# Three row tiles of p @ W_ple_proj computed before v, another order of the products of W_o, and W_up opened by token halves in six chunks

## The chip, the cores and the metric

The kernel runs on one core of a Trainium2 chip. Its engines are TensorE (PE, matmuls; its loads of the stationary operand are shown as PEld), VectorE (DVE), ScalarE (ACT), GpSimd (POOL) and SyncE (SP, which here only issues DMAs). Each engine works through its own instructions in a fixed order and waits for others by semaphores. The metric is the device time of one execution in microseconds (us).

## What is computed

One layer of a decoder: 512 tokens of width 1024, all in float32.

```python
h = rms_norm(x, g_pre_mix)
q, k, v, cb, cc, cu, ga, gc = split(h @ w_in)
y_attn = stick_breaking_attention(q, k, v) @ w_attn_out
y_conv = (cb * causal_depthwise_conv(cc * cu, w_conv)) @ w_conv_out
mixed = (sigmoid(ga + b) * y_attn + sigmoid(gc + b) * y_conv) @ w_o
x = x + rms_norm(mixed, g_post_mix)
f = square(relu(rms_norm(x, g_pre_mlp) @ w_up)) @ w_down      # 1024 -> 4096 -> 1024
x = x + rms_norm(f, g_post_mlp)
x = x + sigmoid(rms_norm(x, g_ple) @ w_ple_gate) * (p @ w_ple_proj)   # p: 512 x 256
```

## The kernel before

**Products.** Each float32 product is made of three matmuls (`mm3`, lines 93 to 95 before, 97 to 99 after): both operands are split into a high part of type fp32r and the rest (`split`: a cast on ACT, line 64 before and 68 after, then a subtraction on DVE, line 65 before and 69 after), and high x high, high x low and low x high are added up in a PSUM bank. A weight chunk therefore needs a DMA into one of four raw buffers (pool `raws`), a cast on ACT and a subtraction on DVE before PE can use it, and the raw buffer is free after the subtraction. PSUM has eight banks, each of 128 x 512.

**Order.** PE and SP run in the order of the source. On ACT, DVE and POOL a scheduler that estimates times sets a fixed order when the program is built; `tc.high_priority(n)` shifts an instruction in its list and `tc.issue_after(i)` keeps one behind another. Each DMA takes one of eight completion semaphores in turn (both SP's and ACT's DMAs), and its issue waits until the DMA that had the same one has landed.

**The head.** SP loads x in four row tiles of 128 tokens (`xin`) and the v columns of w_in in four pieces (`vr`). PE passes the time with transposes of the identity (`warmup`, line 187 before, 208 after), spreads g_pre_mix over the partitions with eight small matmuls (line 228 before, 278 after), transposes the scaled x (`head_turn`, line 206 before, 227 after), and multiplies it with v's columns (`v_mm`). ACT squares x (line 125 before, 129 after), POOL takes the inverse root, DVE scales (`head_scale`, line 196 before).

**W_o.** `mixed @ w_o` is done in 2 x 2 blocks with seven products P1 to P7 in place of eight (a Strassen scheme), each of 24 matmuls of 512 columns in two halves, P6 added onto the bank of P1, P5 onto that of P6, P3 onto that of P5, P4 onto that of P7. Before a product goes onto a bank, ACT copies out what the bank holds (`wo_done`). P3 completes token tiles 0 and 1, P4 completes tiles 2 and 3. After that each tile goes through a chain (`chain_in`, `chain_add`, `chain_out`: square on ACT, inverse root on POOL, multiply and add on DVE, twice), ends in `hn1`, and is transposed on PE by `turn2` (line 570 before) into h2, the input of W_up.

**p @ w_ple_proj.** It does not depend on the rest until the last step. In the kernel before it stands between P4 and W_up: 48 matmuls of 512 columns (`pt`, `wpb`), with `turn2(0)` and `turn2(1)` among them; eight transposes of p stand after the first half of P7. The result goes to DRAM (`pps`) and is read back at the end.

**W_up.** W_up has 32 chunks of 128 columns; chunk c and c + 16 go together. Chunks 0, 16, 1, 17 are done for tokens 0 to 255 first, then for 256 to 511, so that PE can start before tiles 2 and 3 are through their chain (`turn2(2)`, `turn2(3)` stand in the first half). Then chunks 2 and 18 follow with all 512 tokens, and the other 26 chunks in a Strassen scheme of seven products of 12 matmuls with 256 columns for each pair (`up_steps`, `up_mm`), whose weights pass through sums on DVE (lines 781 to 786).

Of the kernel before, what the change touches and what calls it, by code (L numbers as in the profile page):

```python
# [8 lines left out]
F32 = mybir.dt.float32  # L9
# [16 lines left out]
LATE = 150  # L26
EPS = 1e-6
# [6 lines left out]
def hybrid_block(ctx, tc, x, p, g_pre_mix, w_in, b_gate, w_conv, w_attn_out, w_conv_out, w_o,  # L34
# [135 lines left out]

    load_x(0)
# [75 lines left out]
    split_v(1)  # L247
# [317 lines left out]
    def turn2(t):  # L565
        tok = slice(t * P, (t + 1) * P)
        for g in range(2):
            ps = bank()
            for i in range(4):
                nc.tensor.transpose(ps[:, i * P:(i + 1) * P], hn1[t][g][:, i * P:(i + 1) * P], ident)  # L570
            p3 = ps.rearrange("p (a b) -> p a b", b=P)
            hold[:] = split(h2[0][g][:, :, tok], h2[1][g][:, :, tok], p3)
            nc.scalar.copy(hf[t // 2][:, g, :, (t % 2) * P:(t % 2 + 1) * P], p3)
# [5 lines left out]
    ORDER = (1, 2, 6, 7, 5, 3, 4)  # L579
# [29 lines left out]
    pf = {}  # L609

    def load_pp():
        pf[0] = raws.tile([P, NT, 256], F32, tag="raw", name="raw")
        nc.sync.dma_start(pf[0], p[0].rearrange("(t p) d -> p t d", p=P))
        for kk in range(2):
            raw = raws.tile([P, D], F32, tag="raw", name="raw")
            nc.sync.dma_start(raw, w_pp[kk * P:(kk + 1) * P, :])
            split(wpb[kk][:, 0], wpb[kk][:, 1], raw)

    def turn_p():
        for kk in range(2):  # L620
            ps = bank()
            for t in range(NT):
                nc.tensor.transpose(ps[:, t * P:(t + 1) * P], pf[0][:, t, kk * P:(kk + 1) * P], ident)
            split(pt[:, kk], pt[:, 2 + kk], ps)
# [20 lines left out]
    def wo_done(n, t):  # L645
# [8 lines left out]
        elif n == 6:  # L654
            nc.scalar.copy(oc[t + 2][:, 0], ps)
        elif n == 5:
            nc.scalar.copy(oc[t + 2][:, 1], ps)
            nc.vector.tensor_tensor(oc[t + 2][:, 1], oacc[7, t], oc[t + 2][:, 1], op=ALU.add)
        elif n == 3:
            chain_in(t)  # L660
            if t == 1:
                chain_add(0)
                chain_add(1)
                with tc.issue_after(norm[1][1].ins):
                    chain_out(0)
# [24 lines left out]

    pp = [bigt([P, 2, D], F32, "pp") for _ in range(2)]
    for t in range(NT):
        tok = slice(t * P, (t + 1) * P)
        for h_ in range(2):
            cs = slice(h_ * 512, (h_ + 1) * 512)
            ps = bank()
            for kk in range(2):
                mm3(ps, pt[:, kk, tok], pt[:, 2 + kk, tok], wpb[kk][:, 0, cs], wpb[kk][:, 1, cs], kk == 0, kk == 1)
            nc.scalar.copy(pp[t // 2][:, t % 2, cs], ps)
            if (t, h_) in ((0, 1), (1, 0)):  # L700
                turn2(t)
                with tc.issue_after(hold[0].ins), tc.issue_after(hold[1].ins):
                    chain_in(2 + t)
                    chain_add(2 + t)
                    if t == 1:
                        chain_out(2)
                        chain_out(3)
        if t % 2 == 1:
            nc.scalar.dma_start(pps[t // 2], pp[t // 2])
# [116 lines left out]
    for c in (2, 2 + NJ):  # L826
        relu2(c, proj(wcols(w_up, c * P), hm))
# [28 lines left out]
    NI = NJ // 2  # L856
    LEFT = {1: (0, 0), 2: (0, 1), 6: (0, 0), 7: (0, 0), 5: (1, 0), 3: (0, 1), 4: (1, 1)}
# [180 lines left out]
```

## Time and profile before

| what | value |
|---|---|
| median of three runs | 733.33 us (733.2 to 734.62) |
| the profiled execution, its own time | 733.09 us |
| span of that execution, first to last instruction | 731.2 us |
| PE busy | 722.3 us, 99% of the span |
| DVE, ACT, POOL busy | 541.5, 390.4, 110.7 us |
| DMA | 134.38 MB, mean 184 GB/s |

The span leaves out 1.9 us that lie around the instructions. PE's busy time counts from the start of a matmul to its modelled end; since matmuls overlap, 99% says that PE is seldom without an instruction, not that it is at its peak.

### The profile page before, as it was taken

To read this page: it belongs to the slowest core of one execution; us is meant where nothing else is said; L and a number is where in the kernel's file an instruction comes from. 1 tells how busy PE (TensorE), PEld (TensorE's weight loads), DVE (VectorE), ACT (ScalarE), POOL (GpSimd) and SP (SyncE) were. 2 spreads that over 40 slices of the span, in tenths; PEclk is the share of its full clock that TensorE was granted. 3 is DMA by queue.
4 is the path that set the end of the run, shared out by engine and by line. 5 is a ranking of instruction groups with operands and counts; after the bars stand their busy time and mean duration, and the time that the engine had idled before them with its cause. 6 is when DMAs were issued, how large, how long until landed. Compare 5 with 4: busy or idle time off the path is not lost.

```text
span 731.2 us, 10295 instructions
## 1 busy us (share of the span) xinstructions
PE 722.3 (99%) x3964; PEld 626.7 (86%) x3964; DVE 541.5 (74%) x642; ACT 390.4 (53%) x604; POOL 110.7 (15%) x128
## 2 busy tenths in 40 slices
PE   8999999999999999999999999999999999999997
PEld 7888888888888888888999999999988888888886
DVE  5768877879593744978789878876799878369762
ACT  6255455452422222675767667756867476356431
POOL 1106060524353352001100000000000000002100
PEclk9999999999999999999999999999999999999999
DMA  8495717166979989725533344423455766577211
GB/s 317 158 325 151 232 57 228 33 230 200 283 249 293 298 251 336 268 78 176 202 103 108 97 125 121 128 73 103 149 169 188 232 234 221 183 239 283 118 57 58
DMA packets 114233, 134.38 MB, mean 184 GB/s; under 512 B 4196, under 2 KB 82824, under 8 KB 113160
## 3 DMA queue, kind: packets, MB, share of 16 engines
q1 hardware_dynamic: 113592, 129.53, 55.4%
q10 hardware_dynamic: 592, 4.20, 1.4%
q8 instruction: 31, 0.51, 0.3%
q14 instruction: 18, 0.15, 0.1%
HBM read 110.64 MB, written 23.07 MB: 183 GB/s over the span
## 4 chain that ended last, share of the span: by engine, by line
PE 93%; DVE 3%; DMA 2%; ACT 1%; issue 1%; DVEq 0%
PE ps L93 29%; PE ps L95 29%; PE ps L94 29%; DMA raw<-in_w_up_dram 2%; PE ps L391 1%; PE ps L377 1%; PE ps L343 1%; DVE us L65 1%; PE ps L206 0%; PE ps L146 0%; PE ps L187 0%; PE ps L570 0%; ACT us L64 0%; DMA grow<-in_g_pre_mix_dram 0%; DVE s L781 0%
## 5 line engine op out<-in xcount | busy, mean ns | idle before, releaser
L93 PE MATMUL ps<-h1h,whi 128*128 128x512 f32 x288 | 113.3, 393 | 0.0
L95 PE MATMUL ps<-h1h,wlo 128*128 128x512 f32 x288 | 112.2, 390 | 0.0
L94 PE MATMUL ps<-h1l,whi 128*128 128x512 f32 x288 | 112.2, 389 | 0.0
L64 ACT CAST whi<-raw 128x1024 fp32r<-128x1024 f32 (+1 forms) x72 | 58.7, 845 | 68.9 <-DMA raw<-in_w_in_dram 52.0
L65 DVE TENSOR_TENSOR w<-raw,w 128x1024 fp32r<-128x1024 f32 x62 | 75.0, 1221 | 25.0 <-ACT w L64 16.7
L65 DVE TENSOR_TENSOR wlo<-raw,whi 128x1024 fp32r<-128x1024 f32 (+1 forms) x72 | 73.2, 1049 | 22.0 <-ACT whi L64 19.7
L64 ACT CAST w<-raw 128x1024 fp32r<-128x1024 f32 x62 | 64.8, 1052 | 41.6 <-DMA raw<-wsum 17.2
L93 PE MATMUL ps<-w,sb 128*128 128x512 f32 x216 | 84.1, 389 | 0.0
L95 PE MATMUL ps<-w,sb 128*128 128x512 f32 x216 | 84.0, 389 | 0.0
L94 PE MATMUL ps<-w,sb 128*128 128x512 f32 x216 | 84.0, 389 | 0.0
L138 POOL TENSOR_TENSOR rs<-ms,mhalf 128x1 f32<-128x1 f32 x20 | 16.7, 838 | 419.1 <-DVE ms L134 361.2
L93 PEld LDWEIGHTS ps<-h1h,whi 128*128 128x128 f32 x288 | 54.1, 188 | 11.4
L95 PEld LDWEIGHTS ps<-h1h,wlo 128*128 128x128 f32 x288 | 54.1, 188 | 11.3
L94 PEld LDWEIGHTS ps<-h1l,whi 128*128 128x128 f32 x288 | 54.1, 188 | 10.9
L93 PE MATMUL ps<-h2h,us 128*128 128x256 f32 x208 | 59.1, 284 | 0.4 <-DVE tmp L814 0.4
L94 PE MATMUL ps<-h2l,us 128*128 128x256 f32 x208 | 58.8, 283 | 0.0
L95 PE MATMUL ps<-h2h,us 128*128 128x256 f32 x208 | 58.8, 283 | 0.0
L65 DVE TENSOR_TENSOR us<-raw,us 128x1024 fp32r<-128x1024 f32 x39 | 47.4, 1220 | 11.0 <-ACT us L64 11.0
L64 ACT CAST us<-raw 128x1024 fp32r<-128x1024 f32 x39 | 40.2, 1049 | 17.3 <-DVE raw L786 10.2
L94 PEld LDWEIGHTS ps<-w,sb 128*128 128x128 f32 x216 | 40.5, 188 | 8.5
L95 PEld LDWEIGHTS ps<-w,sb 128*128 128x128 f32 x216 | 40.5, 188 | 8.4
L93 PEld LDWEIGHTS ps<-w,sb 128*128 128x128 f32 x216 | 40.5, 188 | 8.3
(221 smaller groups left out, 1718.8 us busy)
## 6 DMA issues: line engine op xcount, KB each, us to landing
raw<-in_w_in_dram SPq DMA_DIRECT2D x36, 512.0 KB, 7.3
w<-in_w_down_dram SPq DMA_DIRECT2D x32, 512.0 KB, 4.5
wsum<-w SPq DMA_DIRECT2D x32, 512.0 KB, 3.4
raw<-in_w_up_dram SPq DMA_DIRECT2D x32, 512.0 KB, 4.3
raw<-wsum SPq DMA_DIRECT2D x32, 512.0 KB, 5.4
raw<-in_w_down_dram SPq DMA_DIRECT2D x24, 512.0 KB, 4.3
raw<-in_w_ple_gate_dram SPq DMA_DIRECT2D x8, 512.0 KB, 6.1
w<-in_w_o_dram SPq DMA_DIRECT2D x6, 512.0 KB, 6.7
```

The source lines that it names most:

```text
L64: a = nc.scalar.copy(hi, src)
L65: b = nc.vector.tensor_tensor(lo, src, hi.bitcast(F32), op=ALU.subtract)
L93: nc.tensor.matmul(ps, lh, rh, start=start, stop=False, skip_group_check=onto)
L94: nc.tensor.matmul(ps, lh, rl, start=False, stop=False, skip_group_check=onto)
L95: nc.tensor.matmul(ps, ll, rh, start=False, stop=stop, skip_group_check=onto)
L138: nc.gpsimd.tensor_tensor(r, m, mhalf, op=ALU.pow)
L343: nc.tensor.matmul(ps[h][:, c0:c0 + n], st[r, a, qb * P:(qb + 1) * P], st[r, b, 0:n], start=i == 0, stop=i == 2)
L377: nc.tensor.transpose(ps[:, c0 + (qb - kb) * P:c0 + (qb - kb + 1) * P], w[:, o:o + P], ident)
L391: nc.tensor.matmul(ps[:, kb * P:S], lhs, wt[i][:, c0:c0 + n], start=(kb == 0 and i == 0), stop=(kb == NT - 1 and i == 1))
```

## The change

- **Head.** p's first three row tiles and all of w_ple_proj are loaded first, ahead of x and v. PE transposes p's tiles (line 246) and multiplies tiles 0, 1 and 2 (`pp_head`, 36 matmuls of 512 columns) before `head_turn(0)`. ACT copies the six banks out and issues three stores to DRAM (line 264). The identity transposes fall from 8 + 12 + 3 to 8 + 4.
- **W_o.** The order becomes P1 P2 P6 P5 P3 P7 P4; weights are prepared three half products ahead, not four. P7 is copied to `tmp` and added from there.
- **Late tile.** Tile 3 of p and w_ple_proj are loaded again during W_o; two transposes after P5 and 12 matmuls after P4 (`pp_late`). `turn2(0)` stands in the middle of P4, `turn2(1)` right after it.
- **W_up.** Chunks 2 and 18 join the four that open by token halves. `turn2(2)` stands after the fourth chunk, `turn2(3)` after the fifth. The copies to `hf` get a lower priority.

```diff
@@ head @@
+AHEAD = 3
+URG = 300
+PUT = 40
+WARM = 4
...
+    load_p(0)
+    for kk in range(2):
+        nc.sync.dma_start(ppr[kk], w_pp[kk * P:(kk + 1) * P, :])
     load_x(0)
+    load_v(0)
+    load_p(1)
     nc.scalar.dma_start(grow[0:NK, 0:P], g_pre_mix.rearrange("o (a b) -> (o a) b", b=P))
     load_x(1)
-    for i in range(4):
+    for i in range(1, 4):
         load_v(i)
...
+    def turn_p(hi, lo, src, n):
+        ps = bank()
+        for kk in range(2):
+            for t in range(n):
+                nc.tensor.transpose(ps[:, (n * kk + t) * P:(n * kk + t + 1) * P], src(t)[:, kk * P:(kk + 1) * P], ident)
+        return split(hi, lo, ps[:, 0:2 * n * P].rearrange("p (a b) -> p a b", a=2))
...
+    def pp_mm(ts, stat, w, to):
+        ps = {(t, h_): bank() for t in ts for h_ in range(2)}
+        for kk in range(2):
+            if kk == 1 and ts[0] == 0:
+                turn_pair(1)
+            for t, h_ in ps:
+                cs = slice(h_ * 512, (h_ + 1) * 512)
+                mm3(ps[t, h_], *(s[:, kk] for s in stat(t)), w[kk][0][:, cs], w[kk][1][:, cs], kk == 0, kk == 1)
+        for t, h_ in ps:
+            nc.scalar.copy(to(t)[:, h_ * 512:(h_ + 1) * 512], ps[t, h_])
+        for t in ts:
+            nc.scalar.dma_start(pps[t // 2][:, t % 2, :], to(t))
...
     warmup(8)
+    turn_pair(0)
...
-    warmup(12)
+    warmup(WARM)
     xs = [xin[t // 2][:, t % 2, :] for t in range(NT)]
-    with tc.issue_after(gdone.ins):
+    for kk in range(2):
+        for h_ in range(2):
+            cs = slice(h_ * 512, (h_ + 1) * 512)
+            ready = split(wpb[kk][0][:, cs], wpb[kk][1][:, cs], ppr[kk][:, cs])
+    pp_head(0, 1)
+    with tc.issue_after(gdone.ins), tc.issue_after(ready[0].ins), tc.issue_after(ready[1].ins):
         rs = {0: rstd_of([xs[0]])}
     scaled = head_scale(0, rs[0])
+    with tc.issue_after(ready[0].ins), tc.issue_after(scaled.ins):
+        split_v(0)
+        last = split_v(1)
     with tc.issue_after(scaled.ins):
         rs[1] = rstd_of([xs[1]])
+    pp_head(2)
     ps0 = head_turn(0)
...
-    warmup(3)
+    vps = [bank(), bank()]
+    v_mm(0, vps[0], 0)
@@ W_o @@
-    ORDER = (1, 2, 6, 7, 5, 3, 4)
+    ORDER = (1, 2, 6, 5, 3, 7, 4)
...
         elif n == 6:
-            nc.scalar.copy(oc[t + 2][:, 0], ps)
+            with tc.high_priority(URG):
+                nc.scalar.copy(oc[t + 2][:, 0], ps)
         elif n == 5:
             nc.scalar.copy(oc[t + 2][:, 1], ps)
-            nc.vector.tensor_tensor(oc[t + 2][:, 1], oacc[7, t], oc[t + 2][:, 1], op=ALU.add)
+        elif n == 7:
+            c = tm()
+            nc.scalar.copy(c, ps)
+            nc.vector.tensor_tensor(oc[t + 2][:, 1], c, oc[t + 2][:, 1], op=ALU.add)
...
-    THEN = {(1, 0): save_sums, (2, 0): load_xr, (2, 1): load_pp, (7, 0): turn_p}
+    THEN = {(1, 0): save_sums, (2, 0): load_xr, (6, 0): load_pp, (5, 1): turn_late,
+            (3, 1): lambda: h2_tiles(), (7, 0): lambda: load_wu(0), (7, 1): lambda: load_wu(NJ),
+            (4, 0): lambda: turn2(0), (4, 1): lambda: (turn2(1), pp_late(), load_wu(1), load_wu(1 + NJ))}
@@ W_up @@
     for half in range(2):
         ns = slice(half * 256, (half + 1) * 256)
-        for c in (0, NJ, 1, 1 + NJ):
+        for c in (0, NJ, 1, 1 + NJ, 2, 2 + NJ):
...
-            if half == 0 and c in (NJ, 1):
-                turn2(3 - c // NJ)
-                if c == NJ:
+            if half == 0 and c in (1 + NJ, 2):
+                turn2(2 if c == 1 + NJ else 3)
+                if c == 1 + NJ:
                     held = list(hold)
...
-    for c in (2, 2 + NJ):
-        relu2(c, proj(wcols(w_up, c * P), hm))
```

**Where it moves instructions.** PE at the start of the program, before: identity, gain, identity, then x's first tile and v (`vh`, `vl` are the split columns of v, `h1h`, `h1l` the split x).

```order
L187 MATMUL ps<-ident 128x128 x8
L228 MATMUL ps<-gsp 128x128 x8
L187 MATMUL ps<-ident 128x128 x12
L206 MATMUL ps<-ident,xin 128x128 x8
L93 MATMUL ps<-vh,h1h 128x512
L94 MATMUL ps<-vl,h1h 128x512
L95 MATMUL ps<-vh,h1l 128x512
L187 MATMUL ps<-ident 128x128 x3
L206 MATMUL ps<-ident,xin 128x128 x8
```

PE at the same place, of the change, up to the first product of p (`wpb` is the split w_ple_proj, `w_108` and `w_109` the split transposed p).

```order
L208 MATMUL ps<-ident 128x128 x8
L246 MATMUL ps<-ident,raw 128x128 x4
L278 MATMUL ps<-gsp 128x128 x8
L208 MATMUL ps<-ident 128x128 x4
L97 MATMUL ps<-wpb,w_108 128x512
L98 MATMUL ps<-wpb,w_108 128x512
L99 MATMUL ps<-wpb,w_109 128x512
```

Such threes stand there twelve times, with two transposes of p's third tile after the fourth; only then x's first tile follows. ACT in the head, of the change, from the first v cast (`vh`) on:

```order
L68 CAST vh<-vr 128x512
L262 COPY pp<-ps 128x512 x2
L264 DMA pps_116<-pp 128x1024
L262 COPY pp<-ps 128x512
L68 CAST vh<-vr 128x512
L264 DMA pps_116<-pp 128x1024
L262 COPY pp<-ps 128x512 x2
L68 CAST h1h<-ps 128x4x128
L264 DMA pps_117<-pp 128x1024
L68 CAST vh<-vr 128x512
L68 CAST h1h<-ps 128x4x128
```

Before, the cast of x's first tile (`h1h`) followed the two squares of x on ACT directly; now six copies and two stores stand between them, and a third store stands right behind it. ACT between P5 and the end of P7, of the change (L733 copies P5's two banks, L129 squares P3's banks and the rows of x, L736 copies P7's banks, `w_3087` and `w_3113` are P4's weights, `whi` W_up's):

```order
L733 COPY w_2861<-ps 128x512
L733 COPY w_2871<-ps 128x512
L68 CAST pt<-ps 128x256
L68 CAST w_3018<-ot 128x1024
L68 CAST w_3034<-ot 128x1024
L68 CAST w_3087<-ot 128x1024
L129 ACTIVATE junk,ss<-ps 128x512
L68 CAST whi<-raw 128x512
L129 ACTIVATE junk,ss<-ps 128x512
L68 CAST whi<-raw 128x512
L68 CAST w_3113<-ot 128x1024
L129 ACTIVATE junk,ss<-xr 128x1024
```

```order
L736 COPY tmp<-ps 128x512
L129 ACTIVATE junk,ss<-xr 128x1024
L718 DMA x1s_2810<-xr 128x2048
L736 COPY tmp<-ps 128x512
```

Before, P7 needed no copy on ACT (DVE added it from its bank after P5), and `pp` products stood on PE between P4 and W_up; now P7's two copies stand between and behind the squares of x's rows.

## Rows read from the trace of the kernel before

**Rows 1.** The page: busy time of each engine, its share of the span, instructions.

```profile
PE 722.3 (99%) x3964; PEld 626.7 (86%) x3964; DVE 541.5 (74%) x642; ACT 390.4 (53%) x604; POOL 110.7 (15%) x128
```

**Rows 2.** Timeline of PE in the first 20 us: start, duration, line, operation, tiles, shape, count, and in brackets the idle time before it and what ended it. Between the rows at 15.48 and 18.88 stand 14 more matmuls of the same shape.

```profile
1.43 1.97 PE L187 MATMUL ps<-ident 128*128 128x128 f32 x8 [1.43 <-POOL ident masks.py:199]
...
5.66 2.82 PE L187 MATMUL ps<-ident 128*128 128x128 f32 x12
...
10.53 0.71 PE L93 MATMUL ps<-vh,h1h 128*128 128x512 f32 x1 [0.34 <-ACT vh L64]
11.34 0.50 PE L94 MATMUL ps<-vl,h1h 128*128 128x512 f32 x1
...
12.23 1.08 PE L206 MATMUL ps<-ident,xin 128*128 128x128 f32 x8
...
15.48 0.39 PE L93 MATMUL ps<-vh,h1h 128*128 128x512 f32 x1
...
18.88 0.39 PE L93 MATMUL ps<-vh,h1h 128*128 128x512 f32 x1
```

**Rows 3.** Timelines of ACT and DVE in the head, columns as in rows 2.

```profile
4.46 1.06 ACT L125 ACTIVATE junk<-xin 128x1024 bf16<-128x1024 f32 x1 [1.54 <-DMA xin<-in_x_dram]
...
9.85 2.18 ACT L64 CAST vh<-vr 128x512 fp32r<-128x512 f32 x4
...
9.99 0.69 DVE L65 TENSOR_TENSOR h1l<-ps,h1h 128x512 fp32r<-128x512 f32 x1 [1.98 <-ACT h1h L64]
```

**Rows 4.** DMA in the head: GB/s in each us of the first 40 us, then the timeline of SP's issues, and the time from issue to landing of the four loads of x (minimum, median, maximum).

```profile
GB/s 0 36 271 401 393 336 367 393 385 414 432 397 406 403 422 351 300 78 0 0 0 16 0 0 0 0 0 0 350 346 326 326 311 395 318 338 295 290 291 289
...
0.80 0.87 SPq L162 DMA_DIRECT2D xin<-in_x_dram  x2
...
3.76 1.04 SPq L162 DMA_DIRECT2D xin<-in_x_dram  x2
...
DMA to landing us min/median/max: 3.6/8.8/9.4
```

**Rows 5.** W_o: timelines of ACT (L655 copies P6, the square is of P3's first bank), PE (`turn2(0)`) and DVE (steps of the chains of tiles 1 and 0), columns as in rows 2.

```profile
319.98 0.59 ACT L655 COPY w<-ps 128x512 f32<-128x512 f32 x1 [1.45 <-PE ps L95]
...
321.42 0.58 ACT L655 COPY w<-ps 128x512 f32<-128x512 f32 x1
321.89 1.06 ACT L64 CAST w<-ot 128x1024 fp32r<-128x1024 f32 x1
322.84 1.05 ACT L64 CAST wpb<-raw 128x1024 fp32r<-128x1024 f32 x1
...
337.19 0.60 ACT L125 ACTIVATE junk<-ps 128x512 bf16<-128x512 f32 x1 [0.21 <-PE ps L95]
...
346.52 1.04 PE L570 MATMUL ps<-ident,w 128*128 128x128 f32 x8
...
342.72 1.29 DVE L537 SCALAR_TENSOR_TENSOR xr<-w,rs,xr 128x1024 f32<-128x1024 f32 x1 [0.45 <-POOL rs L138]
...
344.73 1.29 DVE L540 SCALAR_TENSOR_TENSOR w<-xr,rs,gb 128x1024 f32<-128x1024 f32 x1
```

**Rows 6.** Timeline of PE in the first half of W_up's opening. Between the rows at 363.23 and 365.86 stand 21 more matmuls of this shape.

```profile
363.23 0.28 PE L94 MATMUL ps<-h2l,whi 128*128 128x256 f32 x1
...
365.86 0.28 PE L95 MATMUL ps<-h2h,wlo 128*128 128x256 f32 x1
...
368.15 0.28 PE L95 MATMUL ps<-h2h,wlo 128*128 128x256 f32 x1
368.74 0.39 PE L93 MATMUL ps<-h2h,whi 128*128 128x256 f32 x1 [0.31 <-ACT whi L64]
368.97 0.28 PE L94 MATMUL ps<-h2l,whi 128*128 128x256 f32 x1
369.47 0.39 PE L95 MATMUL ps<-h2h,wlo 128*128 128x256 f32 x1 [0.22 <-DVE wlo L65]
```

**Rows 7.** The Strassen part of W_up: PE's first product of it and its two stalls (timeline), what DVE waited for from 393 to 512 us (total, times, longest), the first one shown with DVE's two instructions after it (timeline), busy us and count of PE, PEld, DVE, ACT and POOL in the stretch 393 to 516 us with PE's granted clock and the DMA engines' share and GB/s, and the piece of the chain that ended last which lies ahead of the first stall (start, us, what).

```profile
393.19 0.28 PE L93 MATMUL ps<-h2h,us 128*128 128x256 f32 x1
...
433.61 0.28 PE L95 MATMUL ps<-h2h,us 128*128 128x256 f32 x1
435.35 0.39 PE L93 MATMUL ps<-tb,us 128*128 128x256 f32 x1 [1.47 <-ACT tmp L812]
...
488.59 0.28 PE L95 MATMUL ps<-tb,us 128*128 128x256 f32 x1
489.30 0.39 PE L93 MATMUL ps<-h2h,us 128*128 128x256 f32 x1 [0.43 <-DVE tmp L814]
...
DVE s L781 <- DMA raw<-in_w_up_dram: 10.7, 7, 2.1
...
403.43 0.69 DVE L781 TENSOR_TENSOR s<-raw 128x512 f32<-128x512 f32 x1 [1.32 <-DMA raw<-in_w_up_dram]
404.04 0.42 DVE L814 TENSOR_TENSOR tmp<-ps,tmp 128x256 f32<-128x256 f32 x1
404.37 1.22 DVE L65 TENSOR_TENSOR us<-raw,us 128x1024 fp32r<-128x1024 f32 x1
...
393.00:516.00 123.00, 121.10 (x1004) 120.48 (x1003) 97.34 (x136) 84.16 (x144) 0.00 (x0) 1.00 0.38 108
...
426.46 5.65 DMA raw<-in_w_up_dram
```

More of the change, by code (lines that the diff above doesn't have):

```diff
@@ L554, in hybrid_block @@
     xr = [bigt([P, 2, D], F32, "xr") for _ in range(2)]
-    pt = bigt([P, 4, S], name="pt")
-    wpb = [bigt([P, 2, D], name="wpb") for _ in range(2)]
     hn1 = {}
-    h2 = hpair("h2")
-    hf = [bigt([P, 2, 4, 256], F32, "hf") for _ in range(2)]
+    h2, hf = ([], []), []
     x1s = [sums.tile([P, 2, D], F32, name=f"x1s{i}") for i in range(2)]
-    pps = [sums.tile([P, 2, D], F32, name=f"pps{i}") for i in range(2)]
     hold = []
@@ L607, in load_xr, with h2_tiles, load_wu @@
             nc.sync.dma_start(xr[t // 2][:, t % 2, :], x[t * P:(t + 1) * P, :])
-    pf = {}
+    late, wu = {}, {}
+    def h2_tiles():
+        for parts in h2:
+            parts.extend(bigt([P, 4, S], name="h2") for _ in range(2))
+        hf.extend(bigt([P, 2, 4, 256], F32, "hf") for _ in range(2))
+    def load_wu(c):
+        if c % NJ == 1:
+            raw = raws.tile([P, NK, P], F32, tag="raw", name="raw")
+            nc.sync.dma_start(raw, w_up[:, c * P:(c + 1) * P].rearrange("(k p) m -> p k m", p=P))
+            hl = bigt([P, 2, NK, P], name="wu")
+            split(hl[:, 0], hl[:, 1], raw)
+            wu[c] = hl[:, 0], hl[:, 1]
+        else:
+            wu[c] = wcols(w_up, c * P)
     def load_pp():
-        pf[0] = raws.tile([P, NT, 256], F32, tag="raw", name="raw")
-        nc.sync.dma_start(pf[0], p[0].rearrange("(t p) d -> p t d", p=P))
+        late['p'] = raws.tile([P, 256], F32, tag="raw", name="raw")
+        nc.sync.dma_start(late['p'], p[0][3 * P:4 * P, :])
+        late['w'] = []
         for kk in range(2):
@@ L616, in load_pp, with turn_late, pp_late @@
             nc.sync.dma_start(raw, w_pp[kk * P:(kk + 1) * P, :])
[L617 to L624, printed above, removed]
+            both = bigt([P, 2, D], name="wpb")
+            split(both[:, 0], both[:, 1], raw)
+            late['w'].append((both[:, 0], both[:, 1]))
+    def turn_late():
+        both = wts.tile([P, 2, 2, P], F32R, tag="w", name="pt")
+        late['t'] = both[:, 0], both[:, 1]
+        turn_p(*late['t'], lambda t: late['p'], 1)
+    def pp_late():
+        to = w4().rearrange("p a b -> p (a b)")
+        pp_mm((3,), lambda t: late['t'], late['w'], lambda t: to)
     oacc, oc, oss = {}, {}, {}
@@ L688, in hybrid_block @@
             THEN[n, i]()
[L691 to L709, printed above, removed]
+    with tc.issue_after(hold[0].ins), tc.issue_after(hold[1].ins):
+        for t in range(2, NT):
+            chain_in(t)
+            chain_add(t)
+        for t in range(2, NT):
+            chain_out(t)
     af = [bigt([P, 4, S], F32, "af") for _ in range(8)]
@@ L856, in hybrid_block @@
     NI = NJ // 2
+    ORDER = (1, 2, 6, 7, 5, 3, 4)
     LEFT = {1: (0, 0), 2: (0, 1), 6: (0, 0), 7: (0, 0), 5: (1, 0), 3: (0, 1), 4: (1, 1)}
```

36 lines of the change are left out of this document (26 added, 10 removed).

## The prediction

> **What bounds the kernel now.** I read the page first: PE is busy 99% of the span and no other engine over 74% [rows 1], so what counts is what PE executes and where it stands still. The timelines of PE show where. In the first 13 us it has little to do: after eight identity transposes come twelve more at 5.66, and v's first product only at 10.53, released by a cast on ACT [rows 2]. After that it runs without a break, one 512-column matmul every 0.227 us (15 starts from 15.48 to 18.88, 3.40 us [rows 2]), to W_up. There are three breaks later: in the opening of W_up, where the next chunk's split is late (three starts from 368.15 to 369.47 take 1.32 where three of 0.12 would take 0.36: 0.96 too much [rows 6]), and twice in the Strassen part (433.61 to 435.35 and 488.59 to 489.30, 1.62 + 0.59 = 2.2 us [rows 7]). So a gain can come from three places only: work moved into the idle head, the 0.96, and the 2.2.
>
> **PE's work, moved.** Between P3's neighbours and W_up, 36 of 48 products of p go away: 36 x 0.227 = 8.17 us. Six of eight transposes of p go too; eight took 1.08 with the last one's tail under the next matmul [rows 2], about 0.11 each: 0.65. Chunks 2 and 18 turn from 48 matmuls of 512 columns into 96 of 256. In the opening 22 starts of 256 columns take 2.63 us (363.23 to 365.86), 0.120 each [rows 6], so 96 x 0.120 - 48 x 0.227 = +0.62. [...]
>
> **The head, step by step.** It now begins with p, w_ple_proj and x.
> - *Loads.* The DMA engines move 271 GB/s in the third us and 336 to 432 after it [rows 4]. x's first tile, 0.52 MB, is there at 4.46 [rows 3]; the fourth, the last of 4.2 MB, is issued at about 4.45 and lands 9.4 later at 13.85 [rows 4]: 3.67 MB in 9.4 us, 390 GB/s. p's three tiles and w_ple_proj add 1.44 MB, 3.7 us. Estimated landings by these rows: p's pair 3.8, w_ple_proj 5.1 and 6.5, x's first tile 7.9, v's first piece 9.3, p's third tile 9.6, x's second 11.0, x's last 17.5.
> - *PE.* Eight identities to 3.4 [rows 2], then at 0.21 each (2.82 for twelve, less the tail) four transposes of p from 3.8 to 4.7, eight gain matmuls to 6.4, four identities to 7.2. w_ple_proj's first casts (0.55 each by the four v casts in 2.18 [rows 3]) and subtractions (0.69) are done by then. So the 36 products begin at about 7.2 in place of 10.53.
> - *Clock.* [...] Dense products now start 3.3 us earlier. If the switch comes 0.5 after the first of them, it is at 7.7; if it stays where it was, at 11.1. I take the middle, 9.4: five products at 0.45, then 31 at 0.227 and two transposes, end at 16.6 (15.7 and 17.5 at the ends).
> - *ACT.* It is the second bound. It waits for x's second tile (11.0) to square it (1.06 [rows 3] and its read-out), casts p's third tile, and then has four copies and two v casts at 0.55: 15.8. The last two copies follow PE's end: 16.6 + 0.6 = 17.2. Only then comes x's first tile (`h1h`, 0.59): 17.75, the subtraction (0.69 [rows 3]) at 18.4; the third matmul of v's first product waits for that, and x's second tile is transposed from 18.65. In the kernel before that stood at 12.23 [rows 2]. With the early switch ACT's queue holds it at 18.2, with the late one it is 19.6.
> - *The third store* takes a completion semaphore that x's last tile has, so ACT stands until that has landed. Alone it would land at 17.5; sharing the engines with two stores for about 0.8 us, at 18.2, 0.45 after ACT is free; two later v splits then come about 0.3 us late. [...] Without it the wait would vanish and the sum be about 0.3 lower; no row here shows a store beside these loads.
>
> v is late by 18.65 - 12.23 + 0.3 less 0.3 of small stalls that are there now: **+6.4** (5.9 to 7.4). It costs less than the 8.82 that moved, because it fills the head.
>
> **W_o.** I walk from P6's end, which ACT's second copy shows at 321.4 [rows 5], with 24 x 0.227 = 5.45 us for a product.
> - P5 goes onto P6's bank 5.45 us sooner than now. ACT copied the first bank at 319.98 to 320.57, and its second at 321.4 to 322.0; P5 needs them at 321.4 and 322.7. Nothing.
> - P3 onto P5's bank: ACT has five casts (0.95 from start to start [rows 5]) between P6's and P5's copies: copy at 326.6 to 327.2; PE is there at 327.0. +0.25.
> - P4 onto P7's bank: the second copy stands behind the square of tile 1's row, which waits for the chain (DVE 1.29 a step, [rows 5]): done at 340.0, wanted at 339.55. With the first one +0.55.
> - `turn2(0)` has 8.2 us of cover after P3, as before (P3's first bank ready 337.19, `turn2(0)` at 346.52, the chain's last step 344.73 + 1.29 = 346.0 [rows 5]). By the same steps it is ready at 340.7, PE comes at 341.4. Nothing, with 0.7 to spare; beyond that every us costs one.
> - W_up's first product waits for the low part of tile 1, which on DVE is behind one chunk's split: +0.3. Later chunks and tiles 2 and 3 are ready 0 to 0.9 us ahead of PE, since the opening is now six chunks (17.3 us a half).
> - The 0.96 at 368 goes: the casts to `hf` that stood before the late chunk now come behind.
>
> From P6's end to the Strassen part: -8.17 - 0.65 - 0.96 + 0.62 + 1.1 = **-8.05**. The 1.1 may be 0.4 to 2.
>
> **Strassen part.** It has the same work. DVE waited 10.7 us in seven waits for raw chunks, up to 2.1 each; the stall at 433.61 hangs on one of them, a DMA of 5.65 us from 426.46 [rows 7]. The order of ACT and DVE is made anew, and the operands come relatively later than before: the first wait shown is at 403.43, 10.2 us after PE's first product [rows 7]; the same sum (`s`) of chunk pair 6 would now stand about 15 us after. Walking on with 1.22, 0.69 and 0.42 us for DVE's steps [rows 7], pair 4 is split 1.0 us ahead of PE, pair 5 four, pair 7 six. With a lead that grows, about half of the stalls should go: **-1.0**, between -2.2 (all gone) and +1.0.
>
> **Sum.** -8.05 + 6.4 - 1.0 = -2.65 on the profiled execution's own 733.09, 1.9 of it outside the span: 730.4. The median of the runs lies 0.24 above that execution, so **730.7**.
>
> **Rivals.**
> 1. *The clock stays low through the products of p.* For it: 8.7 us of transposes did not raise it. Against: it rose within 0.8 of the first 512-column product [rows 2]. If it rose at 14.4 only, 17 products run at 0.45, PE ends at 18.9, v is late by 8.8: 733.3 - 8.05 + 8.8 - 1.0 = 733.1. Chance 0.13.
> 2. *The later stalls move, and do not shrink.* W_o costs 2 and the Strassen part keeps 2.2: -7.15 + 6.4 = -0.75, 732.6. For it: a new order on two engines whose waits are set by DMAs of up to 5.65 us [rows 7]. Chance 0.16.
> 3. *Slower: the first Strassen pairs are late.* The slack of pair 4 is 1.0 us by my walk, and its order puts sums that need PE's second product ahead of pair 4's split on DVE; the chunk loads behind it start later too. If that costs PE what the order has lost against before, 4.8 us, the time is 733.3 - 1.65 + 4.8 = 736.5. It turns the result when the stalls exceed today's by 1.65 + 1.5 = 3.1 us. Against: DVE is busy 97 of the 123 us of this part, ACT 84 [rows 7], so a lost lead is regained. Chance 0.13.
>
> **How the numbers follow.** The forecast holds 0.58 (its own range 728.6 to 731.8: early clock and few stalls at the one end, late clock and W_o at 2 at the other). About 0.2%, 1.5 us, is what a measurement here can tell from no change. Rivals 1 and 2 fall within that, rival 3 beyond it: faster 0.58, same 0.28, slower 0.14. The range leaves out the far end of rival 3 and the case where all stalls go: 728.6 to 734.6.
>
> **What would show it.** Right: products of p on PE from about 7.2 to 16.6 with the first few at half pace; x's second tile transposed near 18.7; v's end 6.4 us later than now and the Strassen part's start about 1.5 us earlier (391.5); PE stalls of some tenths before P3, P4 and W_up, none at the fourth chunk. Wrong: half-pace products beyond 11 us, ACT idle for more than 1 us before a cast of v, a wait of `turn2(0)` on the chain, or PE stalls over 3 us in the Strassen part.

## The result: slower by 0.33%, where faster by 0.36% was forecast

The changed kernel took 735.94 us (median of six runs, 734.89 to 737.67), the kernel before 733.58 in the same comparison: ratio 1.0033, 95% interval 1.0021 to 1.0045. On a second chip it was 735.82 against 732.28: 1.0043 (1.0031 to 1.0055). The forecast was 730.7, its range 728.6 to 734.6.

PE is still the bound, but it now waits more. From the page of the changed kernel, answering to [rows 1]:

```profile
span 734.9 us, 10387 instructions
PE 723.6 (98%) x4001; PEld 628.1 (85%) x4001; DVE 542.8 (74%) x645; ACT 392.8 (53%) x609; POOL 111.4 (15%) x128
```

PE's start times cut the execution at four first products: of `proj_q`, of W_o, of the Strassen part and of W_down. Two executions of each kernel are shown; the last two columns compare the first of each with the forecast.

| stretch (us) | before | before again | changed | changed again | difference | forecast |
|---|---|---|---|---|---|---|
| start to `proj_q` | 36.91 | 36.44 | 44.97 | 44.78 | +8.06 | +6.4 |
| to W_o | 267.92 | 267.92 | 268.20 | 268.11 | +0.28 | 0 |
| W_o and W_up's opening | 88.37 | 88.37 | 81.93 | 81.93 | -6.44 | -8.05 |
| Strassen part | 133.72 | 133.14 | 135.30 | 135.91 | +1.58 | -1.0 |
| from W_down to the end | 204.26 | 204.30 | 204.50 | 204.67 | +0.24 | 0 |

So no single surprise decided it: three terms of the sum missed by 1.7, 1.6 and 2.6 us, all the same way. (The executions under "before" and "changed" differ by 3.5 us in device time, the medians by 2.4, so the table shows more than the typical loss.)

**The head.** Timeline of PE in the changed kernel (start, duration, line, operation, tiles, shape, count, idle time before and what ended it), to be read against [rows 2]:

```profile
7.48 0.77 PE L97 MATMUL ps<-wpb,w 128*128 128x512 f32 x1
8.05 0.63 PE L98 MATMUL ps<-wpb,w 128*128 128x512 f32 x1
...
12.32 0.57 PE L99 MATMUL ps<-wpb,w 128*128 128x512 f32 x1
12.73 0.38 PE L246 MATMUL ps<-ident,raw 128*128 128x128 f32 x2
12.86 0.48 PE L97 MATMUL ps<-wpb,w 128*128 128x512 f32 x1
...
18.42 1.03 PE L227 MATMUL ps<-ident,xin 128*128 128x128 f32 x8
19.74 0.50 PE L97 MATMUL ps<-vh,h1h 128*128 128x512 f32 x1 [0.29 <-ACT h1h L68]
...
20.81 1.03 PE L227 MATMUL ps<-ident,xin 128*128 128x128 f32 x8
```

The products begin at 7.48, but the first twelve run at half pace (from 8.05 to 12.32 ten times 0.427), until 12.7; only then come 24 at 0.227. The last ends near 18.4, and x's second tile is transposed at 20.81 in place of 12.23.

**W_up's first products.** ACT's timeline, then PE's, in the changed kernel:

```profile
350.55 0.59 ACT L68 CAST h<-ps 128x512 fp32r<-128x512 f32 x1 [1.14 <-PE ps L624]
354.40 0.59 ACT L628 COPY hf<-ps 128x512 f32<-128x512 f32 x1 [3.26 <-DVE h L69]
354.88 0.59 ACT L68 CAST h<-ps 128x512 fp32r<-128x512 f32 x1
...
356.79 1.09 ACT L68 CAST h<-ps 128x512 fp32r<-128x512 f32 x2
...
356.93 0.39 PE L99 MATMUL ps<-wpb,pt 128*128 128x512 f32 x1
357.45 0.38 PE L97 MATMUL ps<-h,whi 128*128 128x256 f32 x1
358.58 0.39 PE L98 MATMUL ps<-h,whi 128*128 128x256 f32 x1 [0.75 <-DVE h L69]
```

`hf` keeps h2 in float32 for the Strassen sums. ACT stands 3.26 us at a copy to `hf` that waits for DVE, with the next casts of h queued behind it; PE loses 0.29 and 1.02 us. (A wait of PE is given here as start to start less the cadence; the bracket shows the idle part of it. The start after each wait is some 0.1 late as well.)

**The Strassen part.** ACT, SP, DVE and PE in the changed kernel:

```profile
380.91 0.60 ACT L783 ACTIVATE tmp<-ps 128x512 f32<-128x512 f32 x1 [2.93 <-PE ps L99]
...
383.79 0.60 ACT L783 ACTIVATE tmp<-ps 128x512 f32<-128x512 f32 x1 [1.62 <-PE ps L99]
...
384.95 1.03 ACT L68 CAST us<-raw 128x1024 fp32r<-128x1024 f32 x1
...
393.03 1.50 SPq L834 DMA_DIRECT2D raw<-in_w_up_dram  x2
...
399.97 0.69 DVE L849 TENSOR_TENSOR s<-raw 128x512 f32<-128x512 f32 x1 [1.68 <-DMA raw<-in_w_up_dram]
...
400.91 1.22 DVE L69 TENSOR_TENSOR us<-raw,us 128x1024 fp32r<-128x1024 f32 x1
...
402.18 0.39 PE L99 MATMUL ps<-h,us 128*128 128x256 f32 x1 [0.92 <-DVE us L69]
```

L783 and L784 are a relu step (relu and square of a finished chunk), `s` is a sum that DVE makes of a chunk pair, `us` its split weights. ACT's first cast of pair 3's raw buffers (384.95) stands behind two relu steps that wait for PE, 10.2 us ahead of the Strassen part's first product at 395.11; before had 15.3 (377.89 and 393.19). The loads of pair 5 go out at 393.03, 2 us ahead of that product where before had 7.2. The same cast and loads in before:

```profile
377.89 1.03 ACT L64 CAST us<-raw 128x1024 fp32r<-128x1024 f32 x1
...
385.97 1.50 SPq L766 DMA_DIRECT2D raw<-in_w_up_dram  x2
```

Then DVE, in its fixed order, stands at the sum of a chunk that has not landed, and the split that PE needs is behind it. The view of PE's waits in the changed kernel from 392 to 531 us (total, times, longest):

```profile
PE ps L97 <- DVE tmp L882: 1.3, 2, 0.7
PE ps L97 <- ACT tmp L873: 1.0, 1, 1.0
PE ps L99 <- DVE us L69: 0.9, 1, 0.9
```

Start to start these are 1.08, 1.16, 0.78 and 0.81: 3.8 us, where before had 2.2 [rows 7].

### The profile page after: what moved, and what is told of

Read it like the earlier page. It is cut to its first block, busy times and chain, and to the rows that moved or that the text cites. A ratio compares the mean times of both kernels' runs of the same rounds, so it can differ in the third digit from the quotient of the medians.

```text
span 734.9 us, 10387 instructions
## 1 busy us (share of the span) xinstructions
PE 723.6 (98%) x4001; PEld 628.1 (85%) x4001; DVE 542.8 (74%) x645; ACT 392.8 (53%) x609; POOL 111.4 (15%) x128
## 4 chain that ended last, share of the span: by engine, by line
PE 80%; DVE 10%; DMA 5%; ACT 2%; issue 1%; POOL 0%; DVEq 0%
PE ps L97 25%; PE ps L98 25%; PE ps L99 25%; DMA raw<-in_w_up_dram 4%; DVE us L69 4%; PE ps L447 1%; PE ps L433 1%; PE ps L399 1%; DVE wlo L69 1%; DMA wsum<-w 1%; DVE s L849 1%; DVE raw L853 1%; PE ps L150 0%; POOL rs L142 0%; DVE raw L854 0%
## 5 line engine op out<-in xcount | busy, mean ns | idle before, releaser
L68 ACT CAST whi<-raw 128x1024 fp32r<-128x1024 f32 (+1 forms) x68 | 56.5, 855 | 63.4 <-DMA raw<-in_w_in_dram 49.6
L69 DVE TENSOR_TENSOR wlo<-raw,whi 128x1024 fp32r<-128x1024 f32 (+1 forms) x68 | 69.0, 1045 | 21.6 <-ACT whi L68 18.0
L97 PE MATMUL ps<-h,us 128*128 128x256 f32 x208 | 59.1, 284 | 1.3 <-DVE tmp L882 1.3
L99 PE MATMUL ps<-h,us 128*128 128x256 f32 x208 | 59.0, 283 | 0.9 <-DVE us L69 0.9
L98 PE MATMUL ps<-h,us 128*128 128x256 f32 x208 | 58.8, 283 | 0.0
L68 ACT CAST us<-raw 128x1024 fp32r<-128x1024 f32 x39 | 40.1, 1049 | 19.8 <-DVE raw L854 11.3
```

The source lines that it names most:

```text
L68: a = nc.scalar.copy(hi, src)
L69: b = nc.vector.tensor_tensor(lo, src, hi.bitcast(F32), op=ALU.subtract)
L97: nc.tensor.matmul(ps, lh, rh, start=start, stop=False, skip_group_check=onto)
L98: nc.tensor.matmul(ps, lh, rl, start=False, stop=False, skip_group_check=onto)
L99: nc.tensor.matmul(ps, ll, rh, start=False, stop=stop, skip_group_check=onto)
```

## The experiments

Ratios are to the kernel before on the same chip; the changed kernel itself has 1.0033 and 1.0043. e4 and e8 are one profiled execution each, without a ratio. The edits are shown abridged: `...` and the comments stand for what is left out.

### Relu steps behind pair 3's cast (e1)

```diff
-            if half == 1:
-                relu2(c, ups[c])
+            if half == 1:
+                todo.append(c)
...
+    with tc.issue_after(got[0].ins): [relu2(c, ups[c]) for c in todo]   # got: pair 3's first split
```

> The changed kernel, with one edit: the six relu steps of the opening of W_up are emitted after the first split of chunk pair 3 and may not be issued before its cast on ScalarE. Nothing else is moved by hand. Theory 1 (ScalarE's queue): in the changed kernel the cast of pair 3 stood at 384.95 behind two relu steps that wait for PE, 10.1 us ahead of the Strassen part's first product, where before had 15.3; so raw buffers came free late, the chunk loads of pairs 5 and 6 started late (393.0 and 406.4), and PE waited 1.08 at 400.99 and 1.16, 0.78 and 0.81 later. Then with the edit pair 3's cast comes before 377, the loads of pair 5 start before 387, the wait at 401 is gone, the Strassen part's waits fall from 3.8 us to 0.5 to 2, and the time falls by 2 to 3 us, to 733 to 734. Theory 2 (the chunk loads themselves, 4 to 5.7 us each, set the pace whatever the casts do): the loads start earlier but the waits move to later pairs and keep 3 to 4 us in sum; the time stays within 0.7 us of the changed kernel's.

Ratio 1.0040 (1.0026 to 1.0055), no gain. The chain did move: pair 3's cast at 372.88, pair 5's loads at 385.76, the waits at 401, 448 and 481 gone. But new ones came: 0.93 at 373.4, since that cast now stood between two copies to `hf` whose banks PE wanted, and this:

```profile
397.32 1.04 ACT L68 CAST us<-raw 128x1024 fp32r<-128x1024 f32 x1
...
398.79 0.36 ACT L873 COPY tmp<-ps 128x256 f32<-128x256 f32 x1
...
399.20 0.39 PE L97 MATMUL ps<-tb,us 128*128 128x256 f32 x1 [1.44 <-ACT tmp L873]
```

The copy that frees the bank for PE's next product is now queued behind the crowded relu steps and casts. The Strassen part took 133.58 in place of 135.30, the stretch ahead of it 0.86 more. The cause was right; the cure put the next thing late.

### The casts of h first (e2)

```diff
-            with tc.high_priority(-PUT):
-                nc.scalar.copy(hf[...], p3)
+            pend.append((hf[...], p3))          # flushed behind chunk 16's split
...
-(4, 1): lambda: (turn2(1), pp_late(), load_wu(1), load_wu(1 + NJ))
+(4, 1): lambda: (turn2(1), rest(), pp_late())   # rest: splits of chunks 16, 1, 17
```

> The changed kernel, with the casts around the first two turn2 calls put in another order: the four casts of h come one behind the other, the copies to hf and the splits of chunks 16, 1 and 17 behind them. Theory 1: PE's 1.31 us before the first two products of W_up (357.45 in the changed kernel) came from ScalarE standing 3.26 us at a copy to hf that waited for VectorE, with the next cast of h behind it. With the edit the two waits fall to 0.3 or less, the Strassen part starts 1.0 us earlier relative to W_o, and the time falls by 0.7 to 1.3 us (735 or a little under). Theory 2: VectorE's queue (the chain of tile 1 and the sums of W_o) is what is late, and not ScalarE: then the wait before the first products stays above 0.8 and the time does not move. Theory 3: the wait goes, but PE then only comes earlier to the Strassen part and waits there for the same chunk loads: the start is 1.0 earlier, the Strassen waits 1.0 longer, time unchanged.

Ratio 1.0066 (1.0051 to 1.0081), slower. The 1.31 us before W_up were gone, so theory 1 had the cause; but ACT's squares in the chains of tiles 2 and 3 now stood behind the copies to `hf` and two splits (the first at 359.57, 2.2 us later counted from W_o's start than in the changed kernel), and `turn2(2)` had to wait for its chain. PE's timeline:

```profile
370.11 1.06 PE L624 MATMUL ps<-ident,w 128*128 128x128 f32 x8 [2.57 <-DVE ms L138]
```

That wait cost more than itself: behind it PE ran at a granted clock of 0.50 for 3.4 us, 17 matmuls of 256 columns about 0.21 apart in place of 0.12, 1.5 us more. The view of that stretch (its length; busy us and count of PE, PEld, DVE, ACT and POOL; PE's granted clock; DMA share, GB/s):

```profile
371.50:374.90 3.40, 3.40 (x19) 3.40 (x18) 3.25 (x5) 1.52 (x3) 0.00 (x0) 0.50 0.75 205
```

### The head undone (e3)

```diff
+    load_x(0) ... load_v(3); load_x(2); load_x(3)      # as before
     load_p(0); w_ple_proj; load_p(1)                   # moved behind x and v
...
     v_out(t, ps)
+    pp_head(0, 1); pp_head(2)                          # moved from ahead of v
```

> The changed kernel with its head undone: x and v's columns are loaded first as in the kernel before, twelve warm transposes again, and p and w_ple_proj are loaded behind them; the same 36 products of p stand right behind v, at full pace, ahead of proj_q. W_o's order and W_up's opening stay those of the changed kernel. Theory 1 (the head hid next to nothing, since its products ran at half pace until 12.4 and held up v): x's second tile is transposed at 12.2 to 12.6 in place of 20.8, and the first product of proj_q stands at 36.9 + 36 x 0.227 + 6 x 0.11 + up to 0.6 = 45.7 to 46.4, against 44.97 in the changed kernel; the time is 0.5 to 1.5 us above the changed kernel's. Theory 2 (the prediction's step: filling the head is worth 2.4 us): proj_q starts at 47.3 or later, the time is over 2 us above. Theory 3 (the head cost more than it hid): proj_q starts before 44.9 and the time is lower.

`proj_q` began at 45.19, 8.7 us later than in the two profiles of before's head in which v's first product came as early as here (36.44 and 36.49; 10.07 and 10.11, here 10.08), about what 36 products at 0.227 and six transposes at 0.109 make (8.8). The changed head gave 43.7 to 45.0. So the idle head hid 0.2 to 1.5 us, not 2.4: theory 1. The time, 1.0089 (1.0071 to 1.0108), was higher than that makes it: from `proj_q` to W_o it took 271.71, 3.5 us more than the changed kernel. Two waits of PE from one more queue make 2.2 of that: ACT stood at a cast whose load was late, with the cast of `st` behind it. The other 1.3 are six products of 512 columns behind them at the lower pace, 0.427 apart, from 66.25 on, with a granted clock of 0.50. ACT and PE, then the view of that stretch (columns as in e2):

```profile
61.02 1.05 ACT L68 CAST whi<-raw 128x1024 fp32r<-128x1024 f32 x1 [0.61 <-DMA raw<-in_w_in_dram]
61.98 0.57 ACT L68 CAST st<-ps 128x512 fp32r<-128x512 f32 x1
...
62.60 0.50 PE L398 MATMUL ps<-st 64*128 64x512 f32 x2 [0.93 <-ACT st L68]
63.98 0.50 PE L398 MATMUL ps<-st 64*128 64x512 f32 x2 [0.88 <-DVE st L69]
...
66.25:68.55 2.30, 2.30 (x8) 1.82 (x6) 1.76 (x2) 2.30 (x6) 1.89 (x4) 0.50 0.98 353
```

### Twenty warm transposes (e4), and both kernels once more (e5, e8)

```diff
-WARM = 4
+WARM = 20
```

> The changed kernel with 20 warm transposes in place of 4 ahead of the products of p, so that the first of them comes about 3.4 us later, at 10.9. It tells apart when PE's pace doubles. Theory 1 (the moment does not hang on the products): the pace doubles at 11 to 13 as in the changed kernel, so that 1 to 5 products run at 0.427 in place of 12, and the last product of p ends at 19 to 20. Theory 2 (it follows the first products of 512 columns by some 5 us, as it did from 7.48 to 12.4): it doubles at 15 to 16, again 10 to 12 products run at 0.427, and the last ends at 21 or later.

Theory 1, a little earlier than it says: the pace doubled at 10.6, during the warm transposes, and no product ran at half pace. PE's timeline, and the view of PE's waits from 392 to 531:

```profile
6.71 4.29 PE L208 MATMUL ps<-ident 128*128 128x128 f32 x20
10.75 0.47 PE L97 MATMUL ps<-wpb,w 128*128 128x512 f32 x1
```

```profile
PE ps L97 <- DVE tmp L882: 0.7, 1, 0.7
```

The last product of p ended near 19.3, and `proj_q` began at 45.91, so sixteen more transposes cost 0.9 to 2.2 us. What was not expected: with the order of ACT, DVE, POOL and SP unchanged, the Strassen part waited 1.1 us (start to start) in place of 3.8 and took 132.65. The view of DVE's waits from 395 to 520 us, of the changed kernel and of this one, shows what differed: how long its sums waited for chunk loads (the load that the sum at 446.57 waited for took 6.44 us in the changed kernel, 5.29 here).

```profile
DVE s L849 <- DMA raw<-in_w_up_dram: 11.4, 8, 3.1
```

```profile
DVE s L849 <- DMA raw<-in_w_up_dram: 8.7, 8, 1.9
```

> The changed kernel as it is, once more, on the same chip as the next three, for a second look at what differs from execution to execution. Theory 1 (the moment at which PE's pace doubles and the length of single chunk loads differ from one execution to the next; the four runs so far had the doubling at 9.2, 9.7, 10.6 and 12.7, and Strassen waits of 1.1 to 3.8 us): the doubling lies anywhere from 9 to 13, proj_q's first product stands at 43.5 plus 0.2 for each product at half pace beyond three (43.5 to 45.2), the waits of the Strassen part differ from the 3.8 us of the first profile by 1 us or more, while the waits before P3, P4 and the first two products of W_up are again 0.40, 0.46 and 1.3 within 0.05. Theory 2 (all of it is fixed by the order): doubling at 12.7, proj_q at 45.0, Strassen waits 3.8, each within 0.2. The time is 1.5 to 3.3 us above before's by either.

Theory 1 in the main. The doubling came at 11.7, and the fixed waits were there again: 0.40, 0.45, 0.29 and 1.02. The Strassen waits were 0.93, 1.06, 1.39 and 1.02, 4.4 us. That is 0.6 from the first profile's, where theory 1 asked for 1 or more, and at the same places (PE's waits, 392 to 531):

```profile
PE ps L97 <- DVE tmp L882: 2.1, 2, 1.2
PE ps L97 <- ACT tmp L873: 0.9, 1, 0.9
PE ps L99 <- DVE us L69: 0.8, 1, 0.8
```

> The kernel before as it is, once more, with a profile, to see how much of its waits differs from execution to execution. If the Strassen waits hang on the lengths of single chunk loads, they differ from the 2.2 us of its first profile by 0.5 us or more, at other places; the 0.85 at W_up's fourth chunk, which hangs on the order of ScalarE's casts, is there again. Its head has only one product at half pace wherever the doubling falls between 9 and 12, so proj_q starts at 36.4 to 37.0 in any case.

Before again: `proj_q` at 36.44, 0.85 at W_up's fourth chunk, and 1.62 at 432.93, as in the first profile; the second Strassen wait was 0.24 in place of 0.59. The expectation, waits 0.5 apart and at other places, was wrong.

### Copies to `hf` behind the casts of h (e6)

```diff
+            pend.append((hf[...], p3))
+        if t:
+            with tc.issue_after(hold[0].ins), tc.issue_after(hold[1].ins), tc.high_priority(-PUT):
+                while pend: puts[:] = [nc.scalar.copy(*pend.pop(0))]
```

> The changed kernel, with only the copies to hf of turn2's first two calls moved behind the casts of h of both (on ScalarE, and behind the last low part of h on VectorE); the splits of chunks 16, 1 and 17 keep their place in the program, so that the squares of the chain of tile 2 do not stand behind them as they did in the run with h first. Theory 1: the 1.3 us before W_up's first two products fall to under 0.3 and no wait of turn2(2) takes their place (under 0.5), so the Strassen part starts 1.0 to 1.3 us earlier counted from W_o's first product, and the time is 0.5 to 1.3 us below the changed kernel's on this chip. Theory 2: what is taken away there comes back as a wait of turn2(2) for its chain, or in the Strassen part for the chunk loads: the time is within 0.4 of the changed kernel's.

ACT and PE:

```profile
349.40 1.08 ACT L68 CAST h<-ps 128x512 fp32r<-128x512 f32 x2 [1.14 <-PE ps L624]
353.05 1.07 ACT L68 CAST h<-ps 128x512 fp32r<-128x512 f32 x2 [2.57 <-PE ps L624]
...
356.02 0.28 PE L97 MATMUL ps<-h,whi 128*128 128x256 f32 x1
356.13 0.28 PE L98 MATMUL ps<-h,whi 128*128 128x256 f32 x1
```

The wait before W_up is zero: the copy to `hf` was its cause. But the Strassen part started only 0.39 us earlier counted from W_o, since 1.08 us came back at 370.04, where chunk 2's low part was late, a place that neither theory named; and the Strassen part took 135.55. Ratio 1.0038 (1.0026 to 1.0050): the median is 0.51 us below the changed kernel's, at the edge between the two theories and within the spread of the runs.

### Both edits, each new wait answered (e7), then chunk 2 (e9)

e7 is e6's edit and e1's, and three lines more:

```diff
+                if c == 1 + NJ: held = hold + puts        # pair 3's cast behind turn2(2)'s copies
+    with ..., tc.issue_after(held[2].ins):
+            with tc.high_priority(URG if c == FIRST else 0): nc.scalar.copy(ct[c][0][:, 0:256], ps)
```

> The edit of the run before (copies to hf behind the casts of h) and that of the first experiment (relu steps of the opening behind pair 3's first cast), with two more that answer its two new waits: pair 3's cast waits for turn2(2)'s copy to hf (0.93 us before the second half of W_up), and the copy of the first Strassen product of pair 3 is put ahead of what ScalarE has queued (1.59 us at 397.5). If the waits add up and can be taken away one by one, this kernel loses 1.3 before W_up, and keeps 0.5 to 1.5 of the Strassen waits: 1.5 to 3 us below the changed kernel's time on this chip, and within 0.5 us of before's or up to 1 us faster. If ScalarE's and VectorE's queues only pass the wait on, it is within 0.7 us of the changed kernel's.

Ratio 1.0002 (0.9993 to 1.0012): 732.73 against the changed kernel's 735.82 on the same chip, 3.1 us less. Of the Strassen waits 0.76 us were left, most of it in one (PE's waits from 392 to 531):

```profile
PE ps L97 <- DVE tmp L883: 0.4, 1, 0.4
```

The Strassen part took 132.21. Chunk 2's 1.1 us stayed; e9 loads and splits that chunk ahead of `turn2(2)`:

```diff
+            if half == 0 and c == 1 + NJ: load_wu(2)
```

> The kernel of the run with both edits, and the load and split of chunk 2 stand ahead of turn2(2) in the program, so that ScalarE's second cast of that chunk comes before the casts of h of tile 2. Theory 1: the wait of 1.1 us that the last two runs had at 370 (a product of chunk 2 waiting for the low part, whose cast stood behind the casts of h) is gone or under 0.3, the rest stays, and the time is 0.8 to 1.2 us below that run's, about 1 us (0.1 to 0.2%) faster than before's. Theory 2: the order of all later steps of ScalarE and VectorE is made anew by the edit, and other waits of 0.5 to 1.5 us come up in the Strassen part: the time is within 0.5 of that run's or above.

Ratio 0.9974 (0.9963 to 0.9985): faster than before. W_o and the opening took 80.33, 1.2 less than in e7, as theory 1 has it, and 8.04 less than before; the Strassen part 132.45. Only P3's and P4's waits are left ahead of it (0.39 and 0.49).

### x's first tile ahead of p's third (e10), and the relu edit on the kernel before (e11)

```diff
-    pp_head(2)
     ps0 = head_turn(0)
     head_split(0, ps0, 0)
+    pp_head(2)
```

> The kernel of the run before (chunk 2), and in the head x's first tile is transposed ahead of the products of p's third tile in place of behind them, so that the cast and subtraction of h1 run beside these twelve products. Theory 1 (in the changed head PE waits about 0.5 us for h1's cast and 0.2 to 0.6 for its low part after the last product of p, and x's second tile comes right behind): these waits go, x's second tile is transposed 0.6 to 1.2 us earlier for the same number of half-pace products, and the time is 0.5 to 1.2 us lower. Theory 2: v's casts or loads are the next bound in the head, proj_q starts where it did, and the time stays within 0.4 us.

Ratio 0.9967 (0.9954 to 0.9980), which the runs do not tell from e9's. Theory 2: `proj_q` at 43.78 with five products at half pace, where e2 had 43.68 with five. The wait went to the low part of h1:

```profile
19.26 0.50 PE L99 MATMUL ps<-vh,h1l 128*128 128x512 f32 x1 [0.72 <-DVE h1l L69]
```

> The kernel before, with the same edit of the relu steps (behind pair 3's first cast, and the copy of pair 3's first Strassen product ahead of ScalarE's queue) as the changed kernel had in the run with both. Theory 1 (the Strassen waits of before, 1.6 to 2.2 us in two profiles, also hang on how late pair 3's casts start the chain of buffers and loads): they fall to under 1 us and the kernel is 0.8 to 1.8 us faster than before, so that the edit owes nothing to the change. Theory 2 (in before the lead of 15 us was enough, and its one wait of 1.6 us at 433 hangs on the length of one load): the waits stay within 0.5 of 1.6 to 2.2, and so does the time.

Ratio 1.0004 (0.9996 to 1.0013): theory 2. Pair 3's cast came over 6 us sooner (371.21), and the Strassen part took 134.25; the waits changed places and did not shrink (2.6 us in sum). A longer lead gained before nothing. PE's waits, 392 to 531:

```profile
PE ps L93 <- DVE tmp L814: 1.3, 2, 0.9
PE ps L93 <- ACT tmp L812: 0.5, 1, 0.5
```

## Why the prediction was wrong, step by step

Three steps failed: the moment at which PE's pace doubles in the head, the wait before W_up's first products, and, with the largest miss, the Strassen part, where fewer stalls were forecast and more came. Two of the prediction's own signs of being wrong were seen: products at half pace beyond 11 us, and stalls of over 3 us in the Strassen part.

- **The head, +6.4: too small by 0.8 to 1.7.** Its forecast start of the products (7.2; 7.34 to 7.75 in seven executions) held. The step *Clock* failed: it tied the switch (the moment at which PE's pace doubles) to the first product, took 9.4 with 11.1 as the far end, and the switch came at 12.7 in the profiled execution; the same head had 9.2, 9.7, 10.1, 10.6, 11.7 and 11.9 elsewhere. No run shows that tie, nor the 0.45 for a product ahead of the switch; the runs showed 0.427 there. With four to seven products at half pace `proj_q` began at 43.7 to 44.1, with nine to twelve at 44.6 to 45.0. The row by which rival 1's "against" puts the rise within 0.8 of the first product does not show it: the 0.81 from 10.53 to 11.34 [rows 2] is a wait for v's low part on DVE. Before again has it too (10.07 to 10.88), though there the pace had doubled at 8.4, ahead of any product. In before the switch lies somewhere from 9.8 to 11.3, and rival 1's "against" falls with the row. And even an early switch gave +7.2 (43.7 against 36.4 of before again). The step "the subtraction at 18.4" left out that DVE scales x's second tile (1.40 us) ahead of it: in e1, with the switch at 9.2, the subtraction began 0.45 after the cast of h1, and x's second tile came at 19.66 where 18.65 was forecast. The third store's wait for x's last tile was 0.70 to 1.00 in e1, e2 and e6, where 0.45 was forecast, and none in the profiled execution; what the stores' sharing of the engines had in it, from which the forecast took 0.3, no run shows. Rival 1 had the cause, a late switch, and put it at 14.4. The rows on the switch, PE and DVE in before, then PE in before again:

```profile
8.27 1.91 PE L206 MATMUL ps<-ident,xin 128*128 128x128 f32 x8
...
10.60 0.68 DVE L65 TENSOR_TENSOR vl<-vr,vh 128x512 fp32r<-128x512 f32 x1
```

```profile
8.16 1.15 PE L206 MATMUL ps<-ident,xin 128*128 128x128 f32 x8
...
10.88 0.50 PE L94 MATMUL ps<-vl,h1h 128*128 128x512 f32 x1 [0.31 <-DVE vl L65]
```

- **W_o and the opening, -8.05: right in the work, wrong in one wait.** P3 (0.40 for 0.25), P4 (0.46 for 0.55), `turn2(0)` (none) and the fourth chunk (none) came about as walked. "W_up's first product waits for the low part of tile 1: +0.3" was 1.31: the walk followed DVE, and ACT's copy to `hf`, which stood between two casts of h in its queue, was not in it. That is 1.0 of the 1.6; starts that come a tenth late after each of four waits are most of the rest. With that wait and its successor removed, e9 shows -8.04; that it meets the forecast to 0.01 is partly chance, since there P3, P4 and the late starts behind them make up the 1.1 without a wait of W_up.
- **The Strassen part, -1.0: wrong sign.** "With a lead that grows about half of the stalls should go" failed at its start: the lead was 5 us shorter than in before, since pair 3's cast stood behind relu steps that wait for PE. In the four executions with the relu steps moved (e1, e7, e9, e10) the part took 132.2 to 133.6; in the six without, 134.8 to 135.9 and once 132.7 (e4), so the length of single loads has a share as well. Rival 3 had the mechanism and the place (sums ahead of the split that PE needs, loads later), and priced it at 4.8 us of waits; it was 3.8 and 4.4 in the two profiles. It was given 0.13, because "a lost lead is regained"; in both profiles the waits went on to 492.
- **The gain was there, and small.** With the queues mended, e9 and e10 are 0.26 and 0.33% faster than before, 1.9 and 2.4 us; the forecast was 2.65. The head pays for little of that: e3 puts it at 0.2 to 1.5 us; most is the shorter middle and the waits of W_up and the Strassen part. How much of it the like cures would give before was not run, beyond the relu edit of e11: before's 0.85 at the fourth chunk stands behind a copy to `hf` as well.
- **The range.** Its upper end, 734.6, is about what the far ends of the three terms make together (733.3 - 7.15 + 7.4 + 1.0). In the profile all three lay beyond them (-6.44, +8.06, +1.58), so it was each term's own bound that was too narrow. The copy to `hf` and the relu steps are one cause twice, an order made anew on ACT.

Open: why to W_o 0.2 to 0.3 us was lost (PE's wait at 132 was 0.3 to 0.4 for DVE's `tmp`), what sets the moment at which PE's pace doubles, and what makes single chunk loads longer in one execution than in another.

## What to carry to other kernels

Where a change makes the order of in-order engines anew, read that order around every place where PE has little slack: an instruction that waits for something slow (in the changed kernel a copy 3.26 us for another engine, a relu 2.93 for PE, a sum 1.68 for a load), ahead of a cast or a split that PE needs, is the next stall, and the listing shows it before any run. Take one such wait away and look for what it had hidden: here no cure alone gained more than 0.5 us, four together gained 3.1 (e7), and a fifth took 1.2 more out of its stretch (e9). A wait of PE can also cost more than its length, where the granted clock falls to 0.50 behind it (1.5 us more in e2, 1.3 in e3). Work moved into an idle start is worth what it hides there at the pace PE has then (here 0.427 us a product), not its cost at full pace (0.227).

## What was not expected of the hardware

- The moment at which PE's pace doubles (0.427 to 0.227 us for 512 columns, 0.213 to 0.109 for a transpose) lay at 8.4 to 12.7 us in thirteen executions, and 9.2 to 12.7 for one and the same head. PE had been executing with gaps below 1 us since 1.43 each time, and sixteen more transposes ahead of the products did not delay it (10.6). In before again, e11 and e4 it came during transposes, ahead of any product. The granted clock in the profile reads 1.00 throughout the head, so only the starts of the instructions show it.
- In e2 and e3 PE fell back to the lower pace in mid-kernel, and there the granted clock shows it: 0.50, with products of 512 columns 0.427 apart in e3, the pace of the head. PE had stood 2.57 us in e2, and 0.93 and 0.88 us close together in e3; the 1.47 us of before at 435.35 did not do it (granted clock 1.00 [rows 7]).
- One and the same order waited 1.1, 3.8 and 4.4 us in the Strassen part. Single chunk loads took 3.9 to 6.7 us from issue to landing in these three executions: once a lead is near zero, their length decides what a profile shows.
